# Pacing GpSimd's side work between the forms of the up-projection, four down-projection results with sums of their own, and the gate's row factor by diagonals

## The chip, the cores and the metric

The kernel runs on one core of one Trainium2 chip. A core has TensorE (PE: matmuls, with weight loads PEld beside them), VectorE (DVE), ScalarE (ACT), GpSimd (POOL) and SyncE (SP, which here only issues DMAs). Each engine works through a queue of its own in order, and waits on semaphores for the others. SBUF is the on-chip memory, PSUM the banks that matmuls accumulate in, DRAM tiles (names ending in `_d`) are scratch in device memory. The metric is the device time of one execution in microseconds (us); several runs give a median. One further execution is profiled, and all rows of the profile are from that one.

## The reference

The program computes one step of a decoder trunk with one layer on 1024 prompt tokens and 8 sample tokens (1032 rows of 1024 features), in float32. What matters here is the second half of it:

```python
x = x + jnp.concatenate([o, sg], axis=-1) @ w_out
x = x + jnp.square(jax.nn.relu(rms_norm(x, g_ff) @ w_up)) @ w_down        # w_up 1024x4096, w_down 4096x1024
x = x + (p @ w_ple) * jax.nn.sigmoid(rms_norm(x, g_ple) @ w_ple_gate)     # p has 256 features
y = rms_norm(x, g_final)

def rms_norm(x, gain):
    y = xf * lax.rsqrt(jnp.mean(xf * xf, axis=-1, keepdims=True) + EPS)
    return y * gain
```

The kernel keeps features on partitions and tokens along the free dimension. The normalisation in front of w_up is not applied to the input: squared ReLU scales with the square of its argument, so the product is computed from the unnormalised x, the residual x is multiplied by the token's mean square plus EPS instead, and later factors are set right for it.

## The kernel before, in words

**Arithmetic.** A float32 operand is split into a rounded high part and the rest (`form` for weights: ScalarE makes `whi` at L150, VectorE `wlo` at L153; `split_gain` L166/L167 with a gain for activations). One product is three matmuls: high·high, low·high, high·low. The tokens stand in two sets nn of 516 (512 prompt and 4 sample), and in other places in two column halves t of 256 and 260 per set.

**Up-projection** (about 597 to 937 us on the trace). w_up goes through a seven-product scheme of 2x2 blocks, for 16 column blocks p. For each, TensorE runs 7 products on both t, 168 matmuls (L1184). The weights' combinations s1 to s4 are GpSimd additions (`up_forms`, L1154, L1157, L1160, L1164), each split into high and low parts before its product. The results become four blocks q on VectorE and ScalarE, which also takes ReLU and square (L1211, two passes). `dforms` has GpSimd make four combinations `tt` of the blocks (L1222 to L1224) and SP store all seven as `f_d` in DRAM (L1226, L1227).

Beside it runs `up_rows` as a side task: squares of the residual X1 (ScalarE), their sums (GpSimd L1245), sums over partitions on TensorE (`ms`, L1254), a row of five token tiles through a transpose `msT` and the DRAM tile `row_d` to a broadcast `mb` (`tok_put`, `tok_get`), then 16 products X1·mb (GpSimd L1273), eight differences (L1275) and stores to `x1_d`.

**Down-projection** (about 941 to 1293 us). `down()` goes through four row groups j of w_down, each with seven products in the order P1, P6, P7, P4, P2, P5, P3 (n = 0 to 27). Each has four column blocks p and two t, 96 matmuls (L1416 to L1418) into eight PSUM banks. The activations of a product are one `f_d` row, loaded as `raw` (L1325) and split into `h` by ScalarE and VectorE (L1332, L1333), two products ahead. The weights of a group are quarters A11, A21, A22, A12 (`load_a`, L1340). From them GpSimd makes s1 (L1353), s2 (L1354) for P6 and P5 and the differences `sd` (L1360) for P7 and P3; four forms are kept ahead. VectorE adds each PSUM block into the result tiles named in `INTO` (L1423 copies, L1425 adds). The result tiles start from `x1_d` (`x1_old`, L1369). At j=3 further additions combine the results (L1432 and, after the last product, L1448 to L1450), `gate_in` splits a finished result for the gate, and `add_ss` sums its squares (ScalarE L1378, GpSimd L1379).

**Gate and outputs** (about 1293 to 1457 us). 8 feature blocks m times 4 column blocks of 24 matmuls (`g`, L1614 to L1616) and the embedding product `em`. `p_in` transposes the embedding input `pt` (`pT`, L1523) and splits it (`pp`, L1526, L1527). `rows(nn)` makes the token factor: partition sums `ms`, a Newton inverse square root on VectorE (`rsqrt`, L248 to L254), `msT`, `row_d`, and the broadcast row `rr`. `evg` needs both. `y_out` transposes the results for the last normalisation and stores; its root is taken from ScalarE's table (L261). The two column sets follow each other, and the outputs of the first are woven into the gate of the second.

**What sets the order.** Side tasks are generators: they are woven between TensorE's groups by estimated times that they yield. TensorE's order (in the down-projection SP's too) is the order of the code; the other engines' queues are filled by a scheduler from its own estimate of when things are ready, with priorities (`tc.high_priority`) and `tc.issue_after(instruction)`, which places an instruction behind another.

```python
spawn(up_rows())          # L1283: a side task, "yield 5.0" after each piece
weave(up)
```

## Time and profile before

| | us |
|---|---|
| median of 3 runs | 1456.96 (1453.29 to 1459.82) |
| profiled execution | 1462.3 |
| its span | 1460.6 |
| mean granted TensorE clock | 0.956 |
| TensorE busy | 1324.1 (91%) |
| VectorE / ScalarE / GpSimd busy | 914.0 / 651.7 / 690.9 |

The profiled execution is 5.3 us above the median, and 1.7 us of it lie outside the span. In the rows, a name ahead of `<-` is the output, those behind it are inputs; `x13` counts instructions; "[4.82 <-DMA mb<-row_d]" means that the engine was idle for 4.82 us before and that this DMA ended the wait. A row of waits gives total, times, and the longest. `PEclk` is the granted TensorE clock as a share of full speed. A row of a stretch gives its length, then busy time and instructions of PE, PEld, DVE, ACT and POOL, then PEclk, the share of DMA time and GB/s.

### The profile page before, as it was taken

What the parts mean: (1) busy time and instruction counts of PE and PEld (TensorE: products, weight loads), DVE (VectorE), ACT (ScalarE), POOL (GpSimd) and SP (SyncE); (2) the same over time, 40 slices, a digit from 0 to 9 for tenths busy, and PEclk for the clock granted to TensorE, in tenths of its full rate; (3) what the DMA queues carried; (4) which work ended last, traced back from release to release, by engine and by line L of the source; (5) the groups of instructions that cost most, each with busy time, mean ns of one, the idle gap of its engine ahead of it and who ended that gap; (6) DMA issues with size and microseconds to landing.
All of it is one profiled execution on the core that took longest, in us unless ns stands there. A gap on an engine that the chain in (4) does not pass through costs nothing.

```text
span 1460.6 us, 26483 instructions
## 1 busy us (share of the span) xinstructions
PE 1324.1 (91%) x10183; PEld 1290.2 (88%) x10183; DVE 914.0 (63%) x1832; ACT 651.7 (45%) x1361; POOL 690.9 (47%) x720
## 2 busy tenths in 40 slices
PE   6979977989998999899949999769999999959996
PEld 5979977989898899899949999769999999959995
DVE  7746655366937757465545444456877778984464
ACT  6565646423233227466415544423343333543363
POOL 5300988756415316687686556451515134472110
PEclk9999989999999999999979999989999999989997
DMA  7234525555437612343544444585343423222231
GB/s 242 83 90 133 152 67 165 158 150 155 117 93 209 206 44 59 101 143 127 169 166 139 132 146 146 174 296 196 116 175 116 173 92 143 73 73 66 81 101 59
DMA packets 209695, 194.52 MB, mean 133 GB/s; under 512 B 20547, under 2 KB 183056, under 8 KB 205977
## 3 DMA queue, kind: packets, MB, share of 16 engines
q1 hardware_dynamic: 209568, 192.83, 41.9%
q8 instruction: 80, 1.31, 0.4%
q14 instruction: 47, 0.38, 0.1%
HBM read 132.28 MB, written 60.62 MB: 132 GB/s over the span
## 4 chain that ended last, share of the span: by engine, by line
PE 38%; DVE 7%; POOL 3%; issue 2%; DMA 2%; ACT 1%; SPq 0%; DVEq 0%; POOLq 0%; ACTq 0%
PE d L1417 6%; PE d L1418 6%; PE d L1416 6%; PE A L1184 5%; PE D L1184 3%; DVE wlo L153 2%; PE B L1184 2%; PE g L1614 2%; PE g L1615 2%; PE g L1616 2%; PE C L1184 2%; POOL x L1273 1%; DVE h L1333 1%; DMA a<-in_w_down 1%; DVE yo L1592 0%
## 5 line engine op out<-in xcount | busy, mean ns | idle before, releaser
L209 PE MATMUL g<-ra,whi 128*128 128x384 f32 (+3 forms) x800 | 274.2, 343 | 0.7 <-ACT ra L388 0.6
L1416 PE MATMUL d<-h,whi 128*128 128x260 f32 (+1 forms) x896 | 256.2, 286 | 16.0 <-ACT whi L150 16.0
L1417 PE MATMUL d<-h,wlo 128*128 128x260 f32 (+1 forms) x896 | 257.6, 287 | 8.0 <-DVE wlo L153 7.8
L211 PE MATMUL g<-ra,whi 128*128 128x384 f32 (+3 forms) x800 | 257.6, 322 | 0.8 <-POOL ra L389 0.4
L1418 PE MATMUL d<-h,whi 128*128 128x260 f32 (+1 forms) x896 | 256.7, 286 | 0.0
L210 PE MATMUL g<-ra,wlo 128*128 128x384 f32 (+3 forms) x800 | 256.4, 320 | 0.0
L1416 PEld LDWEIGHTS d<-h,whi 128*128 128x128 f32 x896 | 172.6, 193 | 16.8 <-ACT whi L150 16.7
L1417 PEld LDWEIGHTS d<-h,wlo 128*128 128x128 f32 x896 | 172.2, 192 | 10.3 <-DVE wlo L153 10.3
L1418 PEld LDWEIGHTS d<-h,whi 128*128 128x128 f32 x896 | 172.5, 193 | 0.0
L209 PEld LDWEIGHTS g<-ra,whi 128*128 128x128 f32 x800 | 155.9, 195 | 3.0 <-ACT ra L388 1.0
L211 PEld LDWEIGHTS g<-ra,whi 128*128 128x128 f32 x800 | 154.9, 194 | 2.5 <-POOL ra L389 1.6
L210 PEld LDWEIGHTS g<-ra,wlo 128*128 128x128 f32 x800 | 156.0, 195 | 0.7 <-DVE wlo L153 0.3
L153 DVE TENSOR_TENSOR wlo<-s,whi 128x512 fp32r<-128x512 f32 x96 | 94.0, 980 | 94.9 <-ACT whi L150 94.5
L150 ACT CAST whi<-s 128x512 fp32r<-128x512 f32 x96 | 59.3, 618 | 105.1 <-PE D L1184 26.5
L153 DVE TENSOR_TENSOR wlo<-st,whi 128x512 fp32r<-128x512 f32 x94 | 71.8, 765 | 51.5 <-ACT whi L150 50.9
L1184 PE MATMUL A<-fb,whi 128*128 128x260 f32 (+1 forms) x512 | 97.4, 283 | 0.0
L643 POOL TENSOR_TENSOR it<-ainv,xinv 32x31 f32<-32x31 f32 (+15 forms) x124 | 74.9, 604 | 40.0 <-DMA ainv<-inv_d 30.6
L1211 ACT ACTIVATE q<-q 128x520 f32<-128x520 f32 (+1 forms) x128 | 79.0, 632 | 28.6 <-DVE q L1207 16.5
L1425 DVE TENSOR_TENSOR acc<-acc,d 128x260 f32<-128x260 f32 (+1 forms) x184 | 72.4, 414 | 28.6 <-PE d L1418 25.9
L1332 ACT CAST h<-raw 128x1024 fp32r<-128x1024 f32 (+1 forms) x56 | 57.4, 1054 | 71.8 <-DMA raw<-f_d 37.7
L150 ACT CAST whi<-st 128x512 fp32r<-128x512 f32 x96 | 59.1, 618 | 60.3 <-PE g L211 32.9
L644 POOL TENSOR_TENSOR xinv<-xinv,it 32x31 f32<-32x31 f32 (+15 forms) x124 | 80.8, 652 | 9.6
(427 smaller groups left out, 3526.8 us busy)
## 6 DMA issues: line engine op xcount, KB each, us to landing
raw<-f_d SPq DMA_DIRECT2D x28, 1032.0 KB
a<-in_w_down SPq DMA_DIRECT2D x16, 1024.0 KB
st<-in_w_in SPq DMA_DIRECT2D x24, 512.0 KB
ck<-ck_d SPq DMA_DIRECT2D x32, 320.0 KB
f_d<-tt SPq DMA_DIRECT2D x16, 520.0 KB
ra<-in_w_up SPq DMA_DIRECT2D x32, 256.0 KB
rb<-in_w_up SPq DMA_DIRECT2D x32, 256.0 KB
f_d<-tt SPq DMA_DIRECT2D x16, 512.0 KB
```

The costliest lines, as they stand in the source:

```text
L150: S.copy(dst_hi, src)
L153: lo_eng.tensor_sub(dst_lo, src, f32(dst_hi))
L209: PE.matmul(ps[:, :w], lhsT=whi[k], rhs=xh, start=(k == 0), stop=False)
L210: PE.matmul(ps[:, :w], lhsT=wlo[k], rhs=xh, start=False, stop=False)
L211: PE.matmul(ps[:, :w], lhsT=whi[k], rhs=xl, start=False, stop=(k == nk - 1))
L643: G.tensor_mul(tv, a, x)
L644: G.tensor_sub(X[:, j + 1 :, :w], X[:, j + 1 :, :w], tv)
L1184: PE.matmul(ps, lhsT=a[:, k, :], rhs=x[:, c, k, :], start=(first and k == 0 and j == 0), stop=(k == 3 and j == 2), skip_group_check=True)
L1211: placed["act"] = S.activation(v, v, func).ins
L1416: PE.matmul(ps, lhsT=wh[:, k, :], rhs=xh[:, k, :], start=(k == 0), stop=False)
L1417: PE.matmul(ps, lhsT=wl[:, k, :], rhs=xh[:, k, :], start=False, stop=False)
L1418: PE.matmul(ps, lhsT=wh[:, k, :], rhs=xl[:, k, :], start=False, stop=(k == 3))
```

## The change

Five things are changed; line numbers of the new kernel are in its order rows.

1. **up_rows goes by steps.** It is no longer a side task. `up_stage` advances it by one step (`next(extra, None)`) behind the `dforms` of each (p, t) from p=1 on. A step is two sums, or the partition sums, or both row transposes, or the broadcasts, or one product X1·mb with its store, placed behind the last difference form by `issue_after`. The eight differences L1275 are gone.
2. **The last block of the up-projection** (p=15): its second ReLU and square are one VectorE instruction, and its four `f_d` stores are issued on GpSimd's queue.
3. **Four results, U2 and U3.** P1 and P6 sum into U2 (P1 also into C11), P7 into U3, P4 into C21, P2 into C11, P5 into C12 and C22, P3 into C12. At j=3 all 16 combinations (U3+=U2, C21+=U3, C12+=U2, C22+=U3, four p each) are on GpSimd as their inputs get ready; none is left after the last product.
4. **Loads at the start of the down-projection.** raw comes in two halves; A11, A21, A22 and C11 come first, A12 and C21 after product 0, C12 and C22 after product 1, `pt` after product 10, its scaling at product 14.
5. **The gate's row by diagonals.** `rows_tok(0)` stands in the last product (P3, p=0), `rows_all(0)` behind its p=3: VectorE multiplies the identity by the token factors into five diagonal blocks, TensorE multiplies a matrix of ones by them (`rB`), so that every partition gets the row, and ScalarE copies it into `ss`. No transpose, no DRAM. In `y_out`, nn=0 takes the Newton root.

```diff
-    def tok_put(i, nn, tok):
+    def tok_put(nn, tok):
...
@@ up_stage
-                if name in ("P7", "P3"):
+                if p == 15 and name == "P3":
+                    v = q[:, 0:4:3]
+                    V.scalar_tensor_tensor(v, in0=v, scalar=0.0, in1=v, op0=ALU.max, op1=ALU.mult)
+                elif name in ("P7", "P3"):
...
                     dforms(p, t, q)
+                    if p:
+                        next(extra, None)
...
-        SY.dma_start(f_d[p // 4, 0:3, :, c0 : c0 + w].rearrange("f p c -> p f c"), q[:, 0:3])
-        SY.dma_start(f_d[p // 4, 3:7, :, c0 : c0 + w].rearrange("f p c -> p f c"), tt)
+        (G if p == 15 else SY).dma_start(f_d[p // 4, 0:3, :, c0 : c0 + w].rearrange("f p c -> p f c"), q[:, 0:3])
+        (G if p == 15 else SY).dma_start(f_d[p // 4, 3:7, :, c0 : c0 + w].rearrange("f p c -> p f c"), tt)
@@ up_rows
-                yield 5.0
+                if m % 2 == 0:
+                    yield
...
+        for m in range(KD):
+            for t in range(2):
+                w = WT[t]
                 x = X1[m][:, 512 * t : 512 * t + 2 * w].rearrange("p (a b) -> p a b", a=2)
-                G.tensor_mul(x, x, mb)
-                if m >= 4:
-                    G.tensor_sub(x[:, 0], x[:, 0], x[:, 1])
+                with tc.issue_after(placed["pool"]):
+                    G.tensor_mul(x, x, mbs[t])
                 SY.dma_start(x1_d[m, :, 512 * t : 512 * t + 2 * w].rearrange("p (a b) -> p a b", a=2), x)
-                yield 5.0
+                yield
...
-    INTO = {"P1": (C12, C11), "P6": (C12,), "P7": (P7,), "P4": (P4,), "P2": (C11,), "P5": (P5,), "P3": (P3,)}
+    INTO = {"P1": (U2, C11), "P6": (U2,), "P7": (U3,), "P4": (C21,), "P2": (C11,), "P5": (C12, C22), "P3": (C12,)}
...
+    def rows_tok(ps, nn):
+        tok = toks[:, nn]
+        V.memset(tok, 1.0)
+        for q in range(5):
+            r = rows_of(q)
+            PE.matmul(ps[:r, q : q + 1], lhsT=ss[:, nn, q * P : q * P + r], rhs=ones[:, 0:1], start=True, stop=True)
+        with tc.high_priority(2 * PRI):
+            for r, c in ((P, slice(0, 4)), (TS // 2, slice(4, 5))):
+                V.scalar_tensor_tensor(tok[:r, c], in0=ps[:r, c], scalar=1.0 / D, in1=ems[:r, nn, c], op0=ALU.mult, op1=ALU.add)
+            rsqrt(rsp, tok, tok, "rp")
+            for q in range(5):
+                r = rows_of(q)
+                V.tensor_scalar_mul(sq[:, q * P : q * P + r], ident[:, :r], tok[:, q : q + 1])
+    def rows_all(new, nn):
+        for c in (slice(0, 256), slice(256, 516)):
+            ps = new()[:, : c.stop - c.start]
+            with tc.high_priority(2 * PRI):
+                PE.matmul(ps, lhsT=ones, rhs=sq[:, c], start=True, stop=True)
+                S.copy(ss[:, nn, c], ps)
@@ down
         load_raw(0)
         load_a(0, "A11")
+        load_a(0, "A21")
+        load_a(0, "A22")
         x1_old(C11, 0, 0)
         split_raw(0)
         load_raw(1)
...
-                        add(G, P7, C12)
+                    if name == "P6":
+                        add(U3, U2)
+                    elif name == "P7":
+                        with tc.high_priority(PRI):
+                            add(C21, U3)
                     elif name == "P4":
-                        add(V, P4, P7)
                         gate_in(1, 0, p)
                         add_ss(1, 0, p)
+                        add(C12, U2)
                     elif name == "P2":
                         gate_in(0, 0, p)
                         add_ss(0, 0, p)
+                        add(C22, U3)
+                    elif name == "P3" and p == 0:
+                        rows_tok(psd.tile([P, 512], F32, tag="d", name="ms"), 0)
+                    elif name == "P3" and p == 3:
+                        rows_all(lambda: psd.tile([P, 512], F32, tag="d", name="rB"), 0)
...
-        for p in range(4):
-            G.tensor_add(C12[:, p], C12[:, p], P5[:, p])
-            V.tensor_add(P7[:, p], P7[:, p], P5[:, p])
-            G.tensor_add(C12[:, p], C12[:, p], P3[:, p])
```

GpSimd's queue in the up-projection, before, around the products X1·mb (x is X1, s the weights' sums, tt the difference forms):

```order
L1164 TENSOR_TENSOR s_8530<-rb,s_8411 128x512
L1224 TENSOR_TENSOR tt<-q_6123,tt 128x260
L1273 TENSOR_TENSOR x_5551<-x_5551,mb 128x512
L1273 TENSOR_TENSOR x_5552<-x_5552,mb 128x512
L1273 TENSOR_TENSOR x_5553<-x_5553,mb 128x512 x2
L1273 TENSOR_TENSOR x_5554<-x_5554,mb 128x512 x2
L1273 TENSOR_TENSOR x_5555<-x_5555,mb 128x512
L1273 TENSOR_TENSOR x_5556<-x_5556,mb 128x512
L1273 TENSOR_TENSOR x_5551<-x_5551,mb 128x520
```

The same place in the changed kernel, one whole p-step:

```order
L1164 TENSOR_TENSOR s_9053<-rb,s_8944 128x512
L1228 TENSOR_TENSOR tt<-q_6123,tt 128x256
L1286 TENSOR_TENSOR x_5551<-x_5551,mb 128x512
L1228 TENSOR_TENSOR tt<-q_6123,tt 128x260
L1286 TENSOR_TENSOR x_5551<-x_5551,mb 128x520
L1154 TENSOR_TENSOR s_9167<-rb,ra 128x512
L1157 TENSOR_TENSOR s_9209<-s_9167,ra 128x512
L1160 TENSOR_TENSOR s_9254<-rb,ra 128x512
```

Before, the products stand in a row between two p-steps' forms; now one stands behind each t's last form, and the next step's sums follow.

SP's queue at the passage to the down-projection, before (a_11101 is A11, a_11098 and a_11097 are A21 and A22; the f_d stores are the up-projection's last):

```order
L1325 DMA raw<-f_d 128x2064
L1340 DMA a_11101<-in_w_down 128x4x512
L1226 DMA f_d<-q_6123 128x3x256
L1226 DMA f_d<-q_6123 128x3x260
L1227 DMA f_d<-tt 128x4x256
L1227 DMA f_d<-tt 128x4x260
L1369 DMA acc<-x_d 128x4x256
L1369 DMA acc<-x_d 128x4x260
L1325 DMA raw<-f_d 128x2064
L1340 DMA a_11098<-in_w_down 128x4x512
L1340 DMA a_11097<-in_w_down 128x4x512
```

And in the changed kernel (A11, A21, A22 are a_11092, a_11089, a_11088):

```order
L1340 DMA raw<-f_d 128x1024
L1340 DMA raw<-f_d 128x1040
L1355 DMA a_11092<-in_w_down 128x4x512
L1355 DMA a_11089<-in_w_down 128x4x512
L1355 DMA a_11088<-in_w_down 128x4x512
L1384 DMA acc<-x_d 128x4x256
L1384 DMA acc<-x_d 128x4x260
L1340 DMA raw<-f_d 128x1024
```

The four stores have left SP's queue, and the two quarters stand directly behind the first.

GpSimd's queue in the last row group, j=3, in the changed kernel, behind s1 and s2 (u_11072 is U2, u_11073 is U3; the sd rows are the four forms of P7):

```order
L1375 TENSOR_TENSOR sd<-a_11089,a_11092 128x512
L1472 TENSOR_TENSOR u_11073<-u_11073,u_11072 128x516
L1472 TENSOR_TENSOR acc<-acc,u_11072 128x516
L1375 TENSOR_TENSOR sd<-a_11089,a_11092 128x512
L1472 TENSOR_TENSOR u_11073<-u_11073,u_11072 128x516
L1472 TENSOR_TENSOR acc<-acc,u_11072 128x516
L1472 TENSOR_TENSOR u_11073<-u_11073,u_11072 128x516
L1472 TENSOR_TENSOR acc<-acc,u_11072 128x516
L1375 TENSOR_TENSOR sd<-a_11089,a_11092 128x512
L1472 TENSOR_TENSOR u_11073<-u_11073,u_11072 128x516
L1472 TENSOR_TENSOR acc<-acc,u_11072 128x516
L1472 TENSOR_TENSOR acc<-acc,u_11073 128x516 x2
```

The row behind these is the fourth sd. Before, the four sd forms stood in a row (`L1360`, x4), with the combinations behind them.

More of the change, by code (lines that the diff above doesn't have):

```diff
@@ L1324, in load_raw @@
             j, i = seq[n]
-            SY.dma_start(raw, f_d[j, DSTEPS[i][1]])
+            for c in (slice(0, 1024), slice(1024, 2064)):
+                SY.dma_start(raw[:, c], f_d[j, DSTEPS[i][1], :, c])
     def split_raw(n):
@@ L1513, in p_in @@
                 qs = (q0, q0 + 1) if q0 < 4 else (4,)
[L1514 to L1516 removed]
+                if 4 in qs:
+                    G.tensor_scalar_mul(pt8[nn], pt8[nn], mst[: TS // 2, nn, 4:5])
                 for k in range(2):
@@ L1554, in rows @@
     def rows(nn):
[L1556 to L1569 removed]
+        rows_tok(pss.tile([P, 512], F32, tag="s2", name="ms"), nn)
+        yield 8.0
+        rows_all(lambda: pss.tile([P, 512], F32, tag="s2", name="rB"), nn)
         arrived("r", nn)
@@ L1623, in gate_units @@
                     yield 3 * w * 0.000455
-    held, there = [], set()
+    held, there = [], {("r", 0)}
     def arrived(what, nn):
@@ L1650, in trunk_step_kernel @@
     with tc.manual_schedule(engines={mybir.EngineType.PE}):
-        spawn(rows(0))
         spawn(p_in())
```

133 lines of the change are left out of this document (66 added, 67 removed).

## The prediction

> **What bounds the kernel now.** I read the page's first lines, then stretches of time, TensorE's waits in the up- and down-projection, and last the other engines' rows where TensorE stops.
>
> ```profile
> span 1460.6 us, 26483 instructions
> ## 1 busy us (share of the span) xinstructions
> PE 1324.1 (91%) x10183; PEld 1290.2 (88%) x10183; DVE 914.0 (63%) x1832; ACT 651.7 (45%) x1361; POOL 690.9 (47%) x720
> ```
>
> TensorE is busy for 91% of the span, so time is to be won only where it stands still or runs at a lower clock. In the stretches below, which begin after the work that the change leaves alone, the pairs are busy time and instructions of TensorE, its weight loads, VectorE, ScalarE and GpSimd, followed by the granted clock.
>
> ```profile
> 640.00:690.00 50.00, 50.00 (x422) 50.00 (x421) 29.07 (x48) 30.31 (x59) 37.25 (x30) 1.00 0.41 131
> 700.00:710.00 10.00, 9.53 (x68) 9.19 (x67) 6.81 (x14) 3.96 (x7) 3.54 (x3) 0.83 0.24 78
> 735.00:770.00 35.00, 15.32 (x103) 14.61 (x102) 16.54 (x6) 4.36 (x10) 28.01 (x28) 0.71 0.46 161
> 935.00:950.00 15.00, 7.63 (x48) 7.22 (x47) 8.91 (x10) 6.51 (x10) 7.65 (x6) 0.77 0.39 128
> 955.00:975.00 20.00, 8.85 (x52) 8.35 (x51) 11.04 (x15) 4.49 (x6) 11.99 (x9) 0.68 1.07 370
> 990.00:1000.00 10.00, 7.04 (x45) 6.84 (x46) 7.19 (x10) 3.34 (x6) 2.95 (x2) 0.83 0.43 149
> 1000.00:1050.00 50.00, 49.89 (x418) 49.68 (x417) 37.59 (x60) 18.60 (x26) 18.36 (x12) 1.00 0.45 161
> 1275.00:1293.00 18.00, 15.82 (x113) 14.98 (x113) 16.56 (x25) 4.92 (x9) 14.06 (x10) 0.91 0.18 59
> 1293.00:1320.00 27.00, 12.56 (x89) 11.64 (x88) 20.96 (x40) 15.27 (x29) 15.85 (x12) 0.75 0.29 88
> 1385.00:1405.00 20.00, 17.15 (x143) 16.27 (x142) 14.46 (x41) 17.98 (x34) 2.21 (x3) 1.00 0.37 127
> ```
>
> The first row is full rate: 422 matmuls in 50 us, 8.44 per us. What a stretch lacks of that, divided by 8.44, is its loss, with the low clock in it: 1.9 and 22.8 us in the up-projection, 9.3, 13.8 and 4.7 at the passage to the down-projection, 4.6 and 16.5 around the start of the gate, 3.1 in the first outputs. Together they are 76.7 us, the most that this change could win.
>
> **The up-projection: 24.7 us lost.** TensorE's wait there, GpSimd's rows, and the piece of the chain that follows them:
>
> ```profile
> PE D L1184 <- DVE wlo L153: 14.6, 2, 13.6
> ```
> ```profile
> 726.10 16.80 POOL L1273 TENSOR_TENSOR x<-x,mb 128x512 f32<-128x512 f32 x13 [4.82 <-DMA mb<-row_d]
> 742.86 1.26 POOL L1154 TENSOR_TENSOR s<-rb,ra 128x512 f32<-128x512 f32 x1
> ```
> ```profile
> 744.80 14.12 DVE wlo L153
> ```
>
> Thirteen products run in one piece, and s1, the weight sum that TensorE needs next, comes behind them. Then the split of s1 lasts 14.12 us while GpSimd runs on without a gap (28.01 of 35 us in the stretch). The Trainium skill ("SBUF — State Buffer", section "Practical consequences") has a rule for this pair: a VectorE instruction with two SBUF inputs and a GpSimd instruction that reads SBUF exclude each other for the whole instruction. The 14.12 us row agrees that one of them can be held very long.
>
> The change puts one product behind each half's difference forms. A p-step of 168 matmuls, 20 us, then holds two products of 1.29 (16.80 / 13), 2.6 us, and the eight subtractions are gone. That is not too dense: in the 640–690 stretch, 2.5 p-steps, the squares' sums (some ten, of the products' size) are woven in, GpSimd is busy for 37.25 of 50 us, and TensorE loses nothing. I take the 24.7 us away and leave 1 for the two row transposes, now back to back on one PSUM bank: **−23.7** (bounds −20, if a late form still costs, to −25).
>
> **The passage to the down-projection: 27.8 us lost.** TensorE's longest wait, then the chain, and SP's, VectorE's, ScalarE's and GpSimd's rows there:
>
> ```profile
> PE d L1416 <- ACT whi L150: 16.0, 3, 10.6
> ```
> ```profile
> 945.48 2.99 DMA f_d<-tt
> ...
> 949.99 9.10 DMA a<-in_w_down
> ```
> ```profile
> 942.65 0.36 SPq L1227 DMA_DIRECT2D f_d<-tt  x1
> ```
> ```profile
> 939.92 3.79 DVE L1333 TENSOR_TENSOR h<-raw,h 128x1024 fp32r<-128x1024 f32 x2 [2.31 <-ACT h L1332]
> 943.64 3.56 DVE L153 TENSOR_TENSOR wlo<-a,whi 128x512 fp32r<-128x512 f32 x4
> 948.68 0.42 DVE L1423 COPY acc<-d 128x256 f32<-128x256 f32 x1 [1.48 <-DMA f_d<-tt]
> ```
> ```profile
> 936.22 2.74 ACT L1211 ACTIVATE q<-q 128x512 f32<-128x512 f32 x4 [2.11 <-DVE q L1207]
> ```
> ```profile
> 944.91 0.58 PE L1417 MATMUL d<-h,wlo 128*128 128x256 f32 x1 [3.10 <-DVE wlo L153]
> ```
> ```profile
> 966.78 5.86 POOL L1354 TENSOR_TENSOR s<-s,a 128x512 f32<-128x512 f32 x4
> ```
> ```profile
> 977.91 8.42 POOL L1516 TENSOR_SCALAR pt<-pt,mst 128x256 f32<-128x256 f32 x8
> ```
>
> A21 and A22 are issued behind the last f_d stores on SP's queue, land 9.10 us later, and only then come s1 and s2 (to 972.6). After the change SP holds raw, A11, A21, A22 in a row, and the stores are on GpSimd's queue. First stop: ScalarE's 2.74 us of relu² ahead of the split of raw becomes one VectorE instruction per half, so TensorE starts at 942.3, not 944.9: −2.6. Second: product 0 is 96 matmuls, 11.4 us, plus 1.8 at the low clock, to 955.5; behind it VectorE still has the last evacuations, both h splits (3.79 as above) and the first split of s2 before TensorE goes on, 5 us, to 960.5. Before, the first s2 was finished at 968, split and used at 969.9; of these 9.4 us the start had 2.6, so −6.8 more. Third (4.7 us): the 8.42 us of pt scaling ahead of the sd forms move to product 14, where GpSimd has over half of its time free (18.36 busy of 50): −3.6. Sum **−13**.
>
> A store's issue took SP 0.36 us; no row shows what it takes GpSimd. I bound it from below by that (1.4 for four, in a stretch where GpSimd has nothing else to do) and from above by one of its own additions, 1.3, with which the forms come 5 us later: bound −8. Without the 5 us behind product 0 it is −17. The Trainium skill ("SBUF — State Buffer", section "SBUF: two separate sides") speaks against this edit: descriptors of a DMA on GpSimd's queue are written by GpSimd, and some VectorE instructions can hold that up. If the splits do so (3.79 + 3.56), the stores land about where product 0 ends; no run shows it yet.
>
> **Results with sums of their own.** P5 goes into two results: 8 more evacuations per j. And j=3 has 16 additions of 516 columns, all on GpSimd, where VectorE had eight of its own.
>
> ```profile
> L1425 DVE TENSOR_TENSOR acc<-acc,d x184: 402/414/426, 952.4 to 1269.5; 128x256 f32<-128x256 f32 x92, 128x260 f32<-128x260 f32 x92
> ```
> ```profile
> L1379 POOL TENSOR_TENSOR ss<-ss,sq x14: 1258/1732/2037, 1252.0 to 1314.6; 128x516 f32<-128x516 f32 x14
> ```
> ```profile
> L1360 POOL TENSOR_TENSOR sd<-a,s x16: 1296/1306/2238, 997.2 to 1287.2; 128x512 f32<-128x512 f32 x16
> ```
>
> The evacuations, 32 × 0.41 = 13 us, cost nothing: VectorE has 12.4 of 50 us free (1000–1050); without that cover they would cost up to 13. In GpSimd's order ten additions and three sd forms stand ahead of P7's fourth form, counted from the end of P6's first block. At 1.6 (between 1.3 beside a quiet VectorE and the median of 1.73) and 1.5 these take 20.5, with the form's two casts 1.7 more: 22.2. TensorE is there after six blocks of 24 matmuls (2.85), 17.1: stall **+5** (at 1.3, +1.4; at 2.04, +9). Against it VectorE's eight additions are gone where 4.6 us were lost: −4. Net **+1** (−3 to +6).
>
> **The gate's start: 16.5 us lost.**
>
> ```profile
> 1293.15 0.28 PE L1418 MATMUL d<-h,whi 128*128 128x260 f32 x1
> ```
> ```profile
> 1313.19 0.37 PE L1124 MATMUL msT<-ident,tok 128*5 128x128 f32 x1 [12.70 <-DVE tok L254]
> ```
> ```profile
> L167 DVE SCALAR_TENSOR_TENSOR xt<-acc,vec,xt x8: 741/742/1752, 1297.3 to 1305.8; 128x516 fp32r<-128x516 f32 x8
> ```
> ```profile
> L153 DVE TENSOR_TENSOR wpl<-st,wpl x2: 1208/1209/1210, 1308.9 to 1311.2; 128x1024 fp32r<-128x1024 f32 x2
> ```
>
> TensorE waits 12.7 us for the token factor and goes on 20 us after the last down matmul. In the change the factor is made during P3, and the trip through DRAM is gone. But VectorE's queue behind P3 still holds an evacuation and a weight split (1.5), two wpl splits (2.4), eight xt splits (0.74 to 1.75, taken as 1.1: 8.8) and then the first pp, for which the fifth pT and the first em wait: 13 to 15 us instead of 20. TensorE has some 11 matmuls less to fill the gap with (1.3 us): **−4.5** (−2 at 1.4 each, −9 at 0.74).
>
> **First outputs.** The nn=0 roots leave ScalarE's table:
>
> ```profile
> L261 ACT ACT_TABLE_LOAD x6 | 7.7, 1283 | 0.1
> ```
>
> Five of these loads, and as many back to the sigmoid, stood where 3.1 us were lost: **−1.5** (0 to −3).
>
> **Sum.** −23.7 − 13 + 1 − 4.5 − 1.5 = −41.7. The profiled execution took 1462.3 us (1460.6 of span, 1.7 around it), 5.3 above the median of 1456.96. So about 1420.6 in a profile like it, and **1415** as the median.
>
> **Rivals.** A, VectorE is not what TensorE meets at the two starts: the 5 us behind product 0 go, and most of the gate's 12.7: −42 − 4 − 8, 1403. For it: xt's median of 0.74; against: its 1.75 beside GpSimd. B, GpSimd becomes the bound: additions at 2.04 add 4 at P7, P3's forms behind the later additions 5, the stores' issues 5, late forms in the up-projection 4: 1433. For it: medians of 1.73 when both engines are busy; against: only 14.06 of 18 us busy even there. C, slower: VectorE's first copy of product 0 into U2 waits for the four stores, as the 948.68 row waited for the last. All evacuations and the h splits stand behind it; eight PSUM banks cover TensorE to 955.5, and from there each us of landing is a us lost. To end 0.5% above before, they would have to land 42 + 7 us later, past 1004, 60 us after the issue, against 2.99 on SP's queue. D, the steps do not pace: the first product waits for the broadcast row as before (4.82) or products still gather ahead of s1. With half of the 24.7 us left it is 1427, with all of it 1440.
>
> **Chances.** Forecast 0.70 (1405 to 1425), A 0.09, B 0.11, C 0.04, D 0.06. The good bounds (−25 − 17 − 3 − 9 − 3 = −57) give 1400, the bad ones (−20 − 8 + 6 − 2 = −24) 1433; with most of B and D the range is 1400 to 1436. Within 0.5% (7.3 us, about what a measurement here can tell from no change) lies only a C with landings near 60 us later than now or B and D together, 0.03; slower by more is C's rest and the unforeseen, 0.04; faster 0.93.
>
> **What would show it.** In the profile after: no stretch of 5 us in the up-projection below 41 matmuls and no split over 3 us; a stop of about 5 us behind product 0 that ends on an h or weight split, and none behind the pt scaling; a stop of 1 to 6 us in j=3 at P7's fourth block with GpSimd busy; at the gate a stop that ends on pT or pp. Wrong would be a gap over 10 us in the 700s, GpSimd rows stretched by its DMA issues, or a first copy into U2 that waits for a store far beyond 955.

## The result

| | before | after |
|---|---|---|
| median (us) | 1455.17, 4 runs (1453.29 to 1459.82) | 1420.26, 4 runs (1419.19 to 1421.68) |
| ratio, 95% interval | | 0.9756 [0.9728, 0.9784] |
| profiled execution, span | 1462.3, 1460.6 | 1419.37, 1417.7 |
| mean granted clock | 0.956 | 0.965 |

The change makes the kernel faster by 34.9 us in the medians. The head of the page after:

```profile
span 1417.7 us, 26668 instructions
...
PE 1314.5 (93%) x10189; PEld 1280.7 (90%) x10189; DVE 913.8 (64%) x1900; ACT 638.3 (45%) x1346; POOL 693.4 (49%) x720
```

VectorE and GpSimd are busy for as long as before (914.0 and 690.9 us then). They have not been given less to do; the gain has to be looked for in where their work stands.

Where the time went is read best by stages. Each length below is worked out from the first and last starts of TensorE's instructions: from the span's start to the first up-projection matmul, to the last one, to the last matmul of the down-projection, to the last gate matmul of the first column set, to that of the second, and to the end.

| stage (us) | before | after | difference | forecast |
|---|---|---|---|---|
| ahead of the up-projection | 581.0 | 576.5 | −4.5 | 0 |
| up-projection | 355.9 | 327.3 | −28.6 | −23.7 |
| down-projection | 356.2 | 349.6 | −6.6 | −12 |
| gate, first set | 79.3 | 73.3 | −6.0 | −4.5 |
| gate, second set, and first outputs | 65.1 | 67.4 | +2.3 | −1.5 |
| tail | 23.1 | 23.6 | +0.5 | 0 |
| span | 1460.6 | 1417.7 | −42.9 | −41.7 |

The first row isn't the change: its code is the same. In the profiles of the twelve kernels below, which all share it too, this stage took 574.2 to 582.7 us, while the stages behind it, where their code is the same, repeat within 2.5 us. So the change's own part is −38.4 us, and small edits are compared here by stages rather than by totals.

TensorE's waits in the up-projection after (total, times, longest), and in the stages behind it:

```profile
PE D L1184 <- DVE wlo L153: 0.9, 1, 0.9
PE msT L1124 <- DVE row L1126: 0.6, 1, 0.6
...
PE d L1457 <- DVE wlo L153: 14.3, 9, 6.1
...
PE pT L1579 <- ACT ss L1423: 7.1, 1, 7.1
```

Of the 14.6 us of waits for weight splits in the up-projection 0.9 are left, and the two row transposes cost 0.6. What is left waits for VectorE in the down-projection (L1457 is the old L1417) and for ScalarE at the gate. The stretches after that answer to those before (columns as there):

```profile
640.00:690.00 50.00, 50.00 (x426) 50.00 (x425) 27.55 (x43) 30.29 (x59) 41.52 (x34) 1.00 0.48 147
735.00:770.00 35.00, 35.00 (x299) 35.00 (x298) 17.83 (x33) 18.82 (x36) 21.93 (x18) 1.00 0.52 161
910.00:920.00 10.00, 7.53 (x44) 7.53 (x44) 10.00 (x5) 0.00 (x0) 9.15 (x9) 0.62 1.04 396
903.80:963.80 60.00, 47.18 (x360) 46.56 (x359) 48.32 (x66) 18.70 (x26) 26.50 (x23) 0.89 0.82 290
963.80:1173.80 210.00, 209.51 (x1750) 208.38 (x1749) 173.45 (x300) 80.47 (x110) 74.10 (x52) 1.00 0.43 143
1190.00:1200.00 10.00, 7.46 (x42) 6.99 (x40) 3.73 (x7) 0.66 (x2) 10.00 (x8) 0.71 0.29 99
1200.00:1210.00 10.00, 9.16 (x72) 8.62 (x72) 9.55 (x9) 5.39 (x8) 8.50 (x6) 0.95 0.00 1
1257.00:1285.00 28.00, 20.81 (x156) 19.98 (x157) 17.69 (x34) 17.84 (x39) 12.28 (x11) 0.88 0.14 40
1347.00:1367.00 20.00, 16.68 (x125) 15.80 (x124) 16.54 (x60) 6.44 (x16) 2.19 (x3) 0.91 0.36 121
```

The second row is the place where TensorE had 103 matmuls in 35 us; now it has 299 and the full clock. The fourth begins at the last up-projection matmul. Its counterpart before, and the steady part behind it:

```profile
936.90:996.90 60.00, 38.46 (x262) 37.15 (x261) 34.11 (x50) 17.79 (x25) 31.85 (x26) 0.80 0.66 229
996.90:1226.90 230.00, 229.69 (x1919) 229.07 (x1918) 181.34 (x306) 86.69 (x120) 70.31 (x46) 1.00 0.42 148
```

98 more matmuls in the same 60 us are 98 / 8.44 = 11.6 us won at the passage. The steady part runs at 8.34 per us before (1919 / 230) and 8.33 after (1750 / 210). The down-projection as a whole won only 6.6, so its last row group, j=3, became 5.0 us longer.

The passage and the two places where TensorE stops next (j=3 and the gate), in the order of time:

```profile
905.83 5.45 DVE L1348 TENSOR_TENSOR h<-raw,h 128x1024 fp32r<-128x1024 f32 x2
911.20 9.44 DVE L153 TENSOR_TENSOR wlo<-a,whi 128x512 fp32r<-128x512 f32 x4
912.47 0.58 PE L1457 MATMUL d<-h,wlo 128*128 128x256 f32 x1 [6.12 <-DVE wlo L153]
914.46 5.02 POOL L1368 TENSOR_TENSOR s<-a,a 128x512 f32<-128x512 f32 x4
922.73 5.02 POOL L1369 TENSOR_TENSOR s<-s,a 128x512 f32<-128x512 f32 x4
928.31 2.37 DVE L1348 TENSOR_TENSOR h<-raw,h 128x1024 fp32r<-128x1024 f32 x2
931.34 0.58 PE L1457 MATMUL d<-h,wlo 128*128 128x256 f32 x1 [4.84 <-DVE wlo L153]
...
1189.74 2.30 POOL L1472 TENSOR_TENSOR acc<-acc,u 128x516 f32<-128x516 f32 x1
1192.00 1.26 POOL L1375 TENSOR_TENSOR sd<-a,a 128x512 f32<-128x512 f32 x1
1193.96 0.45 PE L1456 MATMUL d<-h,whi 128*128 128x256 f32 x1 [1.86 <-ACT whi L150]
...
1257.36 3.19 ACT L166 ACTIVATE xt<-acc,vec 128x516 fp32r<-128x516 f32 x5
1260.44 0.35 ACT L1423 COPY ss<-rB 128x256 f32<-128x256 f32 x1
1260.70 1.96 ACT L166 ACTIVATE xt<-acc,vec 128x516 fp32r<-128x516 f32 x3
1262.55 0.36 ACT L1423 COPY ss<-rB 128x260 f32<-128x260 f32 x1
...
1262.97 0.69 PE L1579 MATMUL pT<-ident,pt 128*128 128x128 f32 x2 [7.14 <-ACT ss L1423]
```

Four stops are left: behind the splits of h and of the first quarter (912.47), behind product 0 (931.34), in P7 of j=3 (1193.96, where the third difference form comes late and TensorE then runs at half the clock, 0.71 in the row from 1190 on), and at the gate (1262.97), where the token factor's row is complete on TensorE, but its two copies stand in ScalarE's queue behind five and three gain splits.

### The profile page after: what moved, and what is told of

Its sections match the earlier page's. It is cut to its first block, busy times and chain, and to the rows that moved or that the text cites. A ratio compares the mean times of both kernels' runs of the same rounds, so it can differ in the third digit from the quotient of the medians.

```text
span 1417.7 us, 26668 instructions
## 1 busy us (share of the span) xinstructions
PE 1314.5 (93%) x10189; PEld 1280.7 (90%) x10189; DVE 913.8 (64%) x1900; ACT 638.3 (45%) x1346; POOL 693.4 (49%) x720
## 4 chain that ended last, share of the span: by engine, by line
PE 66%; DVE 11%; POOL 9%; ACT 4%; DMA 3%; issue 3%; SPq 0%; DVEq 0%; POOLq 0%; ACTq 0%
PE A L1184 9%; PE D L1184 6%; PE d L1457 6%; PE d L1458 6%; PE d L1456 6%; PE g L209 5%; PE g L211 5%; PE g L210 4%; PE C L1184 3%; PE B L1184 3%; POOL xinv L644 3%; POOL it L643 3%; DVE wlo L153 2%; PE g L1658 2%; PE g L1659 2%
## 5 line engine op out<-in xcount | busy, mean ns | idle before, releaser
L1457 PE MATMUL d<-h,wlo 128*128 128x260 f32 (+1 forms) x896 | 256.9, 287 | 14.3 <-DVE wlo L153 14.3
L1457 PEld LDWEIGHTS d<-h,wlo 128*128 128x128 f32 x896 | 171.4, 191 | 16.7 <-DVE wlo L153 16.7
L153 DVE TENSOR_TENSOR wlo<-s,whi 128x512 fp32r<-128x512 f32 x96 | 73.7, 769 | 79.9 <-ACT whi L150 79.5
L153 DVE TENSOR_TENSOR wlo<-st,whi 128x512 fp32r<-128x512 f32 x94 | 72.3, 769 | 47.5 <-ACT whi L150 47.0
L150 ACT CAST whi<-st 128x512 fp32r<-128x512 f32 x96 | 59.0, 619 | 67.1 <-PE g L211 32.4
L1348 DVE TENSOR_TENSOR h<-raw,h 128x1024 fp32r<-128x1024 f32 (+1 forms) x56 | 76.8, 1380 | 14.6 <-ACT h L1347 14.5
L1465 DVE TENSOR_TENSOR acc<-acc,d 128x256 f32<-128x256 f32 (+1 forms) x192 | 75.0, 415 | 17.0 <-PE d L1458 16.1
L1214 ACT ACTIVATE q<-q 128x512 f32<-128x512 f32 (+1 forms) x124 | 75.9, 631 | 22.0 <-DVE q L1207 16.1
```

Of the source, the lines that this page charges most:

```text
L150: S.copy(dst_hi, src)
L153: lo_eng.tensor_sub(dst_lo, src, f32(dst_hi))
L1214: placed["act"] = S.activation(v, v, func).ins
L1348: V.tensor_sub(lo[:, c], raw[:, c], f32(hi[:, c]))
L1457: PE.matmul(ps, lhsT=wl[:, k, :], rhs=xh[:, k, :], start=False, stop=False)
```

## The experiments

Each kernel is the changed kernel with one edit, if nothing else is said. No kernel takes back the order of the loads, the four results or the diagonals by itself; what these brought is read from the rows of the two profiles. The stages that the edits touch, in us (for *after* and its repetition, e5, the difference shows what one profile can tell):

| | up | down | gate 1 | gate 2 | median | ratio to before, 95% |
|---|---|---|---|---|---|---|
| after | 327.3 | 349.6 | 73.3 | 67.4 | 1420.26 | 0.9756 [0.9728, 0.9784] |
| e5, the same again | 327.6 | 349.8 | 72.2 | 66.0 | 1421.72 | 0.9735 [0.9704, 0.9765] |
| e1, rows woven | 346.8 | 349.7 | 72.2 | 65.9 | 1440.03 | 0.9842 [0.9810, 0.9875] |
| e2, stores on SP | 327.6 | 352.0 | 71.8 | 67.5 | 1422.62 | 0.9729 [0.9699, 0.9758] |
| e3, root by table | 329.4 | 349.5 | 72.3 | 65.1 | 1420.88 | 0.9714 [0.9689, 0.9739] |
| e4, s1 behind a split | 329.0 | 349.5 | 71.9 | 67.4 | 1420.91 | 0.9714 [0.9687, 0.9741] |
| e6, h split first | 326.9 | 349.0 | 71.6 | 67.1 | 1420.06 | 0.9728 [0.9700, 0.9756] |
| e7, additions behind sd | 329.0 | 347.7 | 72.1 | 67.7 | 1418.71 | 0.9712 [0.9684, 0.9741] |
| e8, pp ahead of xt | 327.1 | 349.5 | 73.6 | 67.3 | 1422.19 | 0.9736 [0.9708, 0.9764] |
| e9, passage kept apart | 327.6 | 346.7 | 72.3 | 67.8 | 1417.35 | 0.9706 [0.9671, 0.9742] |
| e10, j=3 paced | 329.0 | 347.6 | 72.4 | 67.3 | 1418.22 | 0.9712 [0.9682, 0.9743] |
| e11, gain splits paced | 327.3 | 349.6 | 63.9 | 66.4 | 1410.78 | 0.9677 [0.9634, 0.9719] |
| e12, e3 + e9 + e10 + e11 | 327.1 | 344.6 | 62.7 | 66.2 | 1404.66 | 0.9620 [0.9593, 0.9647] |

Kernels e1 to e4 ran beside one set of runs of the kernel before (median 1462.82), e5 to e8 beside a second (1459.82), e9 to e12 beside a third (1460.59).

The up-projection has two lengths in the kernels that keep the steps: 326.9 to 327.6 us, and 329.0 to 329.4 in e3, e4, e7 and e10. In these four the granted clock is at one half for 3.4 us near 705 (e4: 0.83 in the 10 us from 705 on, after: 1.00 in the 10 us from 703 on), which is 1.7 us of full speed.

### e1: the pacing taken back

The row work is a side task again, woven by estimated times; everything else of the change stays.

```diff
-                    if p:
-                        next(extra, None)
...
-        for m in range(KD):
-            for t in range(2):
+        for t in range(2):
+            for m in range(KD):
...
-                with tc.issue_after(placed["pool"]):
-                    G.tensor_mul(x, x, mbs[t])
+                G.tensor_mul(x, x, mbs[t])
...
-    extra = up_rows()
+        spawn(up_rows())
```

> The changed kernel with one part undone: the token squares, row and 16 products run as a side task woven by time again (no steps, no queueing behind the difference forms; the eight subtractions stay out). Theory (products in one piece keep s1 and its split waiting): TensorE stops once in the 700s for 15 to 22 us, a VectorE split there lasts over 10 us, and the time rises by 17 to 25 us over the changed kernel's 1420, to 1437 to 1445. Rival (the up-projection became faster because the eight subtractions and a second partition sum went, or because the profiled execution of before was a slow one): no stop over 5 us, time within 6 us of 1420.

The up-projection took 346.8 us, 19.5 more than after and 17.4 to 19.9 more than the other kernels with the steps; all later stages are as in e5. TensorE's waits in it, and the stretch that was full after:

```profile
PE D L1184 <- ACT whi L150: 8.6, 1, 8.6
PE D L1184 <- DVE wlo L153: 5.5, 2, 4.4
```
```profile
735.00:770.00 35.00, 27.26 (x194) 26.68 (x195) 20.34 (x27) 15.12 (x28) 23.94 (x21) 0.76 0.45 147
```

So 19.5 of the 28.6 us are the steps. The time came as expected, the rows only in part: TensorE's stop is two long waits and not one, and no split lasts over 10 us (the longest of a weight sum is 4.95, at 737.47, where it was 14.12 before). The other 9.1 came with the rest of the change, and two readings of rows cover them: TensorE's waits for weight splits are 14.1 here and were 20.6 before (14.6 and one of 6.0 for `whi`), 6.5 less, and with 426 matmuls per 50 us against 422 at a clock of 1.00 the 2688 matmuls of the up-projection take 3.0 us less. The eight differences (L1275) are gone here too, which fits the shorter waits. But no run separates that, and where the higher rate comes from stays open: in 50 us without a wait of TensorE's every kernel with the steps shows 425 to 427, the only profile of the kernel before 419 to 422.

### e2: the last stores back on SP's queue

```diff
-        (G if p == 15 else SY).dma_start(f_d[...], q[:, 0:3])
-        (G if p == 15 else SY).dma_start(f_d[...], tt)
+        SY.dma_start(f_d[...], q[:, 0:3])
+        SY.dma_start(f_d[...], tt)
```

> The changed kernel with the last four f_d stores back on SP's queue. The order of SP's queue then has one of the four ahead of raw, A11, A21 and A22, and three behind them, ahead of the first results' loads and the second raw. Theory (the load order, not the queue, brings the passage's gain; the stores on GpSimd even take it four issues of 0.8 to 1.0 us each, 3.3 us in a stretch where it is late with s1): within 3 us of the changed kernel, a little faster if anything. Rival (the stores' place decides): raw and the quarters wait for a store that waits for GpSimd's difference forms, TensorE's start of the down-projection is 5 to 10 us later, 1425 to 1430.

```profile
912.43 0.58 PE L1456 MATMUL d<-h,whi 128*128 128x256 f32 x1 [9.54 <-ACT whi L150]
...
918.76 1.09 DVE L1463 COPY u<-d 128x256 f32<-128x256 f32 x3 [3.86 <-DMA f_d<-q]
```
```profile
902.60:962.60 60.00, 45.56 (x339) 44.66 (x338) 40.00 (x65) 20.08 (x27) 23.20 (x19) 0.86 0.90 309
```

The stores on GpSimd's queue are worth 2.4 us: the stage is 352.0 instead of 349.6, and 21 matmuls fewer in the 60 us behind the up-projection say the same (21 / 8.44 = 2.5). The medians are too close to show it. That is the size that was expected, but not the direction, and far less than the rival's 5 to 10. With a store in SP's queue ahead of them, raw and the first quarter come later, and the first copy into U2 waits 3.86 us for a store. That is rival C's mechanism; it appears where the stores are late on SP's queue, and not in the changed kernel. What the stores cost in the changed kernel, from the groups of the store's line L1231 (ns min/median/max, first and last start) and its time to landing:

```profile
L1231 SPq DMA_DIRECT2D f_d<-tt x30: 359/360/578, 606.9 to 894.9; - x30
...
L1231 POOL DMA_DIRECT2D f_d<-tt x2: 769/778/786, 911.8 to 913.7; - x2
...
DMA to landing us min/median/max: 7.4/7.5/7.7
```

Issuing one of these takes GpSimd 0.78 us instead of 0.36, and it lands 7.5 us later, inside the time that product 0 covers. The Trainium skill ("DMA: Bandwidth & Descriptors", section "Anatomy of one DMA — SWDGE (gpsimd) path") fits such a transfer as 2.0 us plus its bytes at 436 GB/s, which would be an estimate of 3.2 us for 520 KB; here, beside the loads of the first weights (396 GB/s in the stretch from 910 to 920), the measured time is more than twice that.

### e3: the first outputs' root from ScalarE's table again

```diff
-                root(st[:r, 0:1], "ry", nn == 1)
+                root(st[:r, 0:1], "ry", True)
```

> The changed kernel with the first outputs' root taken from ScalarE's table again (nn=0 as well). Theory (the Newton root is a chain of eleven small VectorE instructions per output block, each some 0.15 to 0.7 us, in a stretch where TensorE waits for VectorE's scaled outputs): the stretch from the last first-half matmul to the last second-half matmul, 66.9 us in the changed kernel's profile, falls by 2 to 4 us, and the time with it: 1416 to 1418. Rival (as predicted, the table loads are dearer): the stretch grows by 1.5 us, 1421.5.

```profile
1351.00:1371.00 20.00, 17.97 (x152) 17.45 (x151) 13.55 (x39) 15.14 (x27) 3.66 (x5) 1.00 0.41 127
```

Against 125 matmuls in the answering stretch after, the table's version loses 2.0 us there instead of 5.2, and 0.8 in the 20 us ahead of it (162 matmuls) where the Newton version loses none: 2.4 us better, as the stage says (65.1 against 67.4). But the stretch after has a clock of 0.91, and the same Newton code in e5 has 1.00:

```profile
1351.00:1371.00 20.00, 16.69 (x137) 16.01 (x138) 16.77 (x57) 6.78 (x16) 2.68 (x4) 1.00 0.34 116
```

The difference is one stretch of 3.4 us at half the clock (1361.4 to 1364.8 after), 1.7 us of full speed. Of the eleven profiles with the Newton root eight have it (67.1 to 67.8 us) and three don't (e1, e5 and e11, 65.9 to 66.4); the two with the table, e3 and e12 (65.1 and 66.2), don't. So up to 1 us is left for the root itself, and whether the root also makes the slow stretch likelier, two profiles can't tell. The table loads that the edit brings back were not worth 1.5 us on TensorE's path, and the expected fall of the time to 1416 to 1418 did not come (1420.88).

### e4 and e6: which of the engines holds the passage

e4 makes the first s1 wait for VectorE's split of the first quarter's last block, so that the s1 additions and these splits no longer run together. e6 keeps the forms and moves VectorE's evacuations of product 0's third block behind the h splits, those of the fourth behind the first split of s2.

```diff
+                            if j == 0 and p == 0:    # e4: s1 waits for the fourth split of A11
+                                tc.add_manual_dep(i, a11_lo[3].name, ...)
```
```diff
-                    with tc.high_priority(PRI):
...
+                        if n == 0 and p > 1:         # e6
+                            held_back.enter_context(tc.issue_after(placed["h", 1] if p == 2 else placed["s2"]))
```

> The changed kernel with GpSimd's first weight sum of the down-projection (s1, p=0, j=0) made to wait for VectorE's split of the fourth A11 block. Theory (GpSimd's s1 and the difference forms run beside VectorE's splits of raw and A11 and stretch the four weight splits from 3.6 to 9.4 us; TensorE in product 0 waits for them): the four splits take 3 to 4.5 us, product 0 runs 5 us earlier, s1 starts at about the same time or a little later, and product 1 starts 0 to 4 us earlier: 1416 to 1420. Rival (s2's forms set product 1's start and s1 now starts later): the splits shorten, product 1 starts 1 to 5 us later, 1421 to 1425.

> The changed kernel with VectorE's queue in product 0 of the down-projection reordered: the evacuations of the third block come behind the h splits for product 1, those of the fourth block behind the first split of s2. Theory (the stop of 4.8 us behind product 0 is VectorE's queue order: the h splits and the s2 split stand behind the last evacuation although raw came 8 us earlier): the stop falls under 1 us and the down-projection from 349.6 to 344 to 346 us. Rival (s2 itself, finished by GpSimd only about 928, or the first results' loads, set product 1's start): the stop shrinks by at most 2 us and may move into product 0: 348 to 351 us.

e4:

```profile
916.55 3.93 DVE L153 TENSOR_TENSOR wlo<-a,whi 128x512 fp32r<-128x512 f32 x4
...
936.33 0.58 PE L1464 MATMUL d<-h,wlo 128*128 128x256 f32 x1 [4.84 <-DVE wlo L153]
```

The four splits take 3.93 us instead of 9.44, so GpSimd's additions beside them cost them 5.5 us. But TensorE's stop behind product 0 is the same 4.84, the stage the same 349.5. So the stretched splits don't set the end of product 0, against the expectation that it would run 5 us earlier. What fits is that it runs at a low clock (0.62 in the stretch from 910 to 920 after, 0.64 from 915 to 925 here) and takes each split late anyway.

e6:

```profile
928.45 6.98 POOL L1369 TENSOR_TENSOR s<-s,a 128x512 f32<-128x512 f32 x4
929.07 4.00 DVE L1348 TENSOR_TENSOR h<-raw,h 128x1024 fp32r<-128x1024 f32 x2
...
936.03 0.39 PE L1459 MATMUL d<-h,wlo 128*128 128x256 f32 x1 [3.85 <-DVE wlo L153]
```

The stop falls by 1.0 us only. The h splits start earlier and now meet GpSimd's s2: 4.00 us instead of 2.37 for them, 6.98 instead of 5.02 for the four s2. So e4 takes away a meeting of the two engines that did not set the stop, and e6 makes a new one.

### e9: the two kept apart behind product 0

Both edits, and s2 from its second block on waits for the h split.

```diff
+                                if p == 0:
+                                    tc.add_manual_dep(i1, a11_lo[3].name, sync, reason="s1 late")
+                                else:
+                                    tc.add_manual_dep(i2, placed["h", 1].name, sync, reason="s2 late")
```

> The changed kernel, passage to the down-projection only: VectorE's queue as in the run with the h splits first, and GpSimd held apart from it: s1 waits for the fourth A11 split, the second to fourth s2 form wait for product 1's h splits. Theory (in the run with the h splits first the stop behind product 0 only shrank to 3.9 us because h's splits and s2 then ran at the same time and took 4.0 and 7.0 us instead of 2.4 and 5.0): with the two engines apart the splits take 2.4 and 2.6 us, the stop behind product 0 falls under 1.5 us, the down-projection from 349.6 (and 349.0) to 344.5 to 347 us. Rival (s2's later forms now come too late, since they wait for h): the stop goes to product 1's second block, 348 to 351 us.

```profile
927.28 3.72 DVE L1348 TENSOR_TENSOR h<-raw,h 128x1024 fp32r<-128x1024 f32 x2
...
933.02 0.39 PE L1469 MATMUL d<-h,wlo 128*128 128x256 f32 x1 [1.60 <-DVE wlo L153]
```
```profile
908.60:968.60 60.00, 49.46 (x388) 48.63 (x387) 47.62 (x71) 20.03 (x28) 28.01 (x23) 0.91 0.81 291
```

The stop is 1.60 us, 28 matmuls more fit into the 60 us (3.3 us), and the stage is 2.9 us shorter. So the stop behind product 0 was VectorE's queue, as the forecast had it, together with GpSimd's forms, and 3 of its 5 us can be had. Two meetings are left: the h splits of product 0 still run beside GpSimd's last difference forms and store issues (5.45 us for two, from 910.61 on, as after), so TensorE's first stop is unchanged, and those of product 1 still overlap the first s2 (3.72 us for two).

The Trainium skill ("SBUF — State Buffer", section "Who interferes with whom") names this pair: a VectorE instruction with two SBUF inputs contends with a GpSimd instruction that reads SBUF. The splits of 9.44 us beside s1 and of 3.93 us behind it agree.

### e7 and e10: the additions of j=3

e7 places the four C12 += U2 behind the last form of P7. e10 does that for the first of them, and places the others, and the C22 += U3, one by one behind the sum of squares of each p.

```diff
-                        add(C12, U2)
+                        with tc.issue_after(placed["ss"] if p else placed["sd"]):   # e7: placed["sd"]
+                            add(C12, U2)
...
-                        add(C22, U3)
+                        with tc.issue_after(placed["ss"]):                          # e10 only
+                            add(C22, U3)
```

> The changed kernel with the four additions C12+=U2 of j=3 queued on GpSimd behind the fourth sd form of P7. Theory (ten 516-wide additions ahead of that form are the stop at 1190 to 1200, with its half clock): the stop at P7's fourth and at P4's first block shrinks from 5 to 7 us to under 2 and the down-projection from 349.6 to 344 to 346 us. Rival (the U3 additions and the C21 additions alone, or VectorE's load in that stretch, keep the form late, or the additions moved back stop P3's forms instead): 348 to 351 us with a stop of the same size somewhere in j=3.

> The changed kernel, j=3 only: C12+=U2 behind the fourth sd of P7 and then one behind each of P4's sums of squares, C22+=U3 one behind each of P2's. Theory (with the four additions moved as a block the P7 stop went, but GpSimd's runs of 10.4 and 10.3 us without a gap doubled VectorE's splits from 0.7 to 1.46 us and VectorE became full from 1200 to 1240; one addition per 2.85 us block leaves gaps): down-projection from 347.7 to 343 to 346 us, no stop over 2 us in j=3. Rival (VectorE's own load, not the gaps, fills it: the sum of squares and an addition per block keep GpSimd just as busy): 346.5 to 349 us.

Three stretches of j=3 in e7, and the last of them in e10:

```profile
1180.00:1200.00 20.00, 20.00 (x170) 20.00 (x170) 16.91 (x23) 8.28 (x12) 19.37 (x13) 1.00 0.26 78
1200.00:1220.00 20.00, 17.12 (x144) 16.91 (x143) 20.00 (x21) 9.60 (x15) 18.18 (x12) 1.00 0.25 70
1220.00:1240.00 20.00, 18.33 (x132) 18.33 (x133) 20.00 (x34) 10.29 (x16) 8.63 (x6) 0.83 0.12 38
```
```profile
1220.00:1240.00 20.00, 16.22 (x121) 16.01 (x122) 20.00 (x28) 9.49 (x15) 14.67 (x9) 0.91 0.08 26
```

The same by products, from the start of a product's first matmul to that of the next (for P3 to its last matmul), in us:

| j=3 | P1 | P6 | P7 | P4 | P2 | P5 | P3 |
|---|---|---|---|---|---|---|---|
| before | 11.5 | 11.4 | 11.5 | 11.4 | 11.5 | 11.8 | 16.1 |
| after | 11.4 | 11.5 | 18.4 | 11.5 | 12.1 | 12.8 | 12.4 |
| e7 | 11.4 | 11.5 | 11.4 | 11.5 | 18.5 | 11.7 | 12.4 |
| e10 | 11.4 | 11.5 | 11.4 | 11.5 | 15.4 | 15.0 | 12.4 |

In e7 the stop in P7 is gone (170 matmuls in the first 20 us), but the additions now stand in two runs of six (10.39 and 10.32 us on GpSimd) and VectorE, beside them, has no free time from 1200 to 1240. The loss moves to P2; 1.9 us of it stay won. e10 takes the runs apart and gains no more (347.6 against 347.7): the loss stands in P2 and P5 (121 matmuls from 1220 to 1240), and VectorE is still full there. e10's rival came (346.5 to 349); e7's 347.7 lies between its theory (344 to 346) and its rival (348 to 351). Pacing GpSimd alone does not empty VectorE's queue in j=3. Whether VectorE's own evacuations, splits and gain splits fill it, or GpSimd's share of stretching them, no run separates: a weight split there still takes up to 1.78 us (at 1223.76 in e10) where others take 0.68.

### e8 and e11: what holds the gate's start

e8 places the second half's gain splits and squares behind the first casts of the embedding input (`pp`). e11 places each block's gain splits and squares behind the sigmoid and product of the latest gate block, and spaces them wider.

```diff
-                gate_in(ab, 1, p)
-                add_ss(ab, 1, p)
+                with tc.issue_after(placed["pp", 0]):        # e8
+                    gate_in(ab, 1, p)
+                    add_ss(ab, 1, p)
```
```diff
+                with tc.issue_after(placed["sig"]), tc.issue_after(placed["evg"]):   # e11
+                    gate_in(ab, 1, p)
+                    add_ss(ab, 1, p)
-                yield 2.0
+                yield 3.0
-        spawn(second_half(), 6.0)
+        spawn(second_half(), 9.0)
```

> The changed kernel with ScalarE's gain splits and squares of the second column set queued behind the embedding input's casts (pp) of the first set. Theory (the stop at the gate's start, 7.1 us on the copy of the broadcast row out of PSUM, is ScalarE's queue: two copies and the pp casts stand behind eight gain splits, and then between squares that wait for GpSimd): TensorE's stop falls to 2 to 4 us, what is left being the wait for the w_ple weights, and the first half of the gate from 73.3 to 64 to 68 us. Rival (VectorE's splits, as the prediction has it, bound the stretch): the stop moves to VectorE's pp or xt splits, 71 to 74 us, or the second half gets longer by what the first wins.

> The changed kernel, gate only: the eight gain splits and squares of the second column set are queued one behind each gate block's sigmoid and product, from about 9 us after the gate's start. Theory (the run with pp ahead of xt cured the first stop, 7.1 to 1.1 us, and got a new one of 6.3 us, on VectorE's pp for the second set behind eight gain splits in a row of up to 1.5 us: a queue, not the work, is what TensorE waits for): the stop is under 2 us in all, the first half of the gate falls from 73.3 (and 73.6) to 64 to 68 us, the second half stays at 66 to 68. Rival (VectorE is full in this stretch, so the wait comes back at the gate's evacuations, or the second set's factor is late and the second half gets longer): gate as a whole (139 to 141 us in both halves) within 2 us.

e8, a row of time and the group of VectorE's gain splits:

```profile
1276.21 0.66 PE L1579 MATMUL pT<-ident,pt 128*128 128x128 f32 x2 [6.32 <-DVE pp L1583]
```
```profile
L167 DVE SCALAR_TENSOR_TENSOR xt<-acc,vec,xt x8: 740/742/1758, 1267.4 to 1274.0; 128x516 fp32r<-128x516 f32 x8
```

TensorE's first stop is 1.14 us instead of 7.14, and 17 us later it stops for 6.32: the eight gain splits now stand in one run ahead of the next `pp`. The stage is 73.6, no gain. e11:

```profile
1257.37 0.44 PE L1579 MATMUL pT<-ident,pt 128*128 128x128 f32 x2 [1.39 <-ACT ss L1423]
```
```profile
1257.00:1285.00 28.00, 27.63 (x226) 27.00 (x227) 18.19 (x35) 15.63 (x35) 10.94 (x11) 1.00 0.24 69
```

226 matmuls instead of 156 in the 28 us, at a clock of 1.00 instead of 0.88, and the stage takes 63.9 us, 9.4 less than after. The gate's loss was the sixteen gain splits and the squares that stood in a row on two engines, whichever of TensorE's inputs they stood ahead of; one block at a time between the gate's own work they cost nearly nothing.

### e12: together

e3, e9, e10 and e11 in one kernel.

> All of it: the passage apart, j=3 paced, the gain splits paced, and the first outputs' root from the table. If the parts add up (down 349.6 to about 341, first half of the gate 73 to 66, second half 67 to 65) the span is 1420 less 17, about 1403; with the rivals of the three single runs it stays within 5 us of 1420. The parts lie in different stages, so the stage lengths should be those of the single runs within 2 us.

1404.66 us (1402.68 to 1406.61, 5 runs), 0.962 [0.9593, 0.9647] of the kernel before: faster than both, by 17 us than the changed kernel in e5. Down-projection 344.6 (−5.0 to after), first set of the gate 62.7 (−10.6), second 66.2. The first is the sum of e9 and e10 (2.9 + 2.0) and short of the expected 341; the second is e11's 9.4 and 1.2 more.

## Why the prediction was right, and where it wasn't

The forecast was 1415 with 1400 to 1436, the measured median is 1420.26. The sum was −41.7; the stages behind the unchanged first one gave −38.4, 3.3 less, and that puts the median at 1418.6 (1456.96 − 38.4) or, from the median over four runs, 1416.8. The rest, 1.7 to 3.5 us, is inside the spread of the kernel before's runs (6.5). The sum came nearer than its terms: −28.6 for −23.7 on one side, +5.0 for +1 and +2.3 for −1.5 on the other. That part of the hit is luck.

**The up-projection, −23.7: right in kind, too small.** The rows came as said: the stretch that had lost 22.8 us is at full rate, the split of s1 that took 14.12 us is gone (the longest split of a weight sum after is 1.44), and the row transposes cost 0.6 for the forecast 1. Behind the first 13 us of the stage, slow before too, only the 5 us around the transposes have fewer than 41 matmuls (37 from 703 to 708). The stage gave −28.6. The pacing, to which the term gave nearly all, is 19.5 of it by e1; of the other 9.1 the term held nothing apart from the subtractions. 3.0 of them are the yardstick: 8.44 matmuls per us, taken from the kernel before, was not the full rate after (8.52).

**The passage, −13: measured −11.6, and its three parts differ more than their sum.** The first was wrong. "So TensorE starts at 942.3, not 944.9: −2.6" gives 5.4 us behind the start of the last up-projection matmul, 936.9; measured are 8.7 (903.8 to 912.47), against 8.0 before (936.9 to 944.91), so +0.7. ScalarE's relu² did leave the path, but it stands on VectorE now, ahead of the two h splits, and these take 5.45 us for 3.79. The longer one is the first (3.77 us from 905.83 on, 2.11 before); difference forms and store issues (0.97 and 0.79 us) take turns on GpSimd in that time, and no run separates the two. The second came in kind, a stop of 4.84 us behind product 0 for 5: TensorE goes on 27.5 us behind the last up-projection matmul, 33.0 before, which is −6.2 behind the late start, for −6.8. The third, with no stop left behind the pt scaling, is −6.2 for −3.6 by the start of product 3 (63.6 us behind the last up-projection matmul before, 51.9 after). The clock is in it: behind the second stop it stayed at one half for 6.1 us before (969.9 to 976.0) and for 3.4 after (931.3 to 934.7).

**j=3, +1: measured +5.0.** By products, "−4" came: P3, beside which the eight additions had stood, is 3.7 us shorter (16.1 to 12.4), though no run tests that they were the cause. The steps that failed are the stall, "+5", and a term that was put at nothing. P7 is 6.9 us longer. Its stop comes one form earlier than worked out: already the third form waits, behind four additions that took 7.7 us on GpSimd (1.9 each, for the 1.6 of the sum), and TensorE then runs at half the clock until the fourth. P2 and P5 are 1.6 us longer together, where the evacuations and the later additions were to cost nothing; TensorE waits there for VectorE's splits, and VectorE is busy for 19.67 of 20 us from 1220 to 1240. e7 and e10 take the stop in P7 away, and most of the loss comes back further on, on VectorE. The whole term lies inside its bounds of −3 to +6.

**The gate, −4.5: measured −6.0, by another way.** "A stop that ends on pT or pp" with VectorE's queue as the cause was the forecast. The stop does end on pT, but its releaser is ScalarE's copy of the row, behind eight gain splits of ScalarE. VectorE's queue, which the forecast priced, is what comes next: e8 removes the first stop and meets exactly that, 6.32 us on `pp` behind eight `xt`. The size was right by luck: both queues hold the same eight blocks.

**First outputs, −1.5: +2.3, and no gain in any profile.** 1.7 of the 2.3 are the stretch at half the clock (e3). Five table loads left ScalarE, which was not what TensorE waited for; the Newton steps went to VectorE, whose `yo` TensorE waits for.

**The rivals.** A didn't come by itself: both starts end on a queue, and e9 and e11 show 3 and 9 us there, for the forecast 4 and 8. B: GpSimd's forms were late at P7 only, 6.9 us for the forecast's 5 and B's 9. C: the first copy into U2 waited for no store; its mechanism shows in e2. D: the steps paced.

## What to carry to other kernels

Work that must run beside TensorE on an engine with a queue of its own belongs between that engine's urgent instructions one piece at a time, on every queue that it touches: pacing GpSimd's products was worth 19.5 us here, pacing ScalarE's and VectorE's gain splits another 9.4, while moving the same run as a whole (e7, e8) moved the stop and won 1.9 us at most. A form on GpSimd and a two-input split on VectorE slow each other, so the place to win is where they don't meet. And edits of 2 or 3 us are told from stage lengths in the trace, not from totals that vary by 8.5 us in a stage that the edit doesn't touch.

## What the runs showed of the hardware that was not expected

A store issued on GpSimd's queue took that engine 0.78 us for 0.36 on SP, and landed 7.5 us later, against 2.99 for the last one on SP's queue before. It was still the better queue, since the loads that TensorE needs no longer stood behind it (e2).

The stretching beside GpSimd goes both ways and depends on the pairing: four splits took 9.44 us beside four s1 that kept their 5.02, so there VectorE alone paid, but the h splits and s2 in e6 both paid (4.00 for 2.37, 6.98 for 5.02).

The part of the program that all kernels share varied by 8.5 us between profiles (574.2 to 582.7), and that is most of the variation from run to run that the profiles show; its cause was not looked for. Most of the rest are single stretches of 3.4 us at half the granted clock, which stand in some profiles of the same code and not in others: near 705 in four of the twelve kernels with the steps, and in the first outputs in eight of the eleven with the Newton root.
